# Output projection of a hybrid encoder layer as a Strassen product over pairs of T tiles

## The chip, the cores and the metric

The kernel runs on one core of a Trainium2 chip. The metric is device time in microseconds (us). Three runs of the kernel before took 2392.14 (median), 2390.62 and 2395.7 us. One more execution was profiled.

## The reference

One encoder layer in float32, T = 2048 tokens, width 1024, batch 1. The stages up to the FFN, cut:

```
hmix = rms_norm(x, g_norm1) * (1 + scale1) + shift1
q_a,k_a,v_a, q_m,k_m,v_m, o_m, gates = split(hmix @ w_in)
att = rms_norm(banded_attention(q_a, k_a, v_a, sink), g_attn_out)          # 512 columns
h_m = sigmoid(o_m) * rms_norm(h_fwd + h_bwd, g_mlstm_out)                  # 512 columns
mix = concatenate([att, h_m], axis=-1) @ w_out                             # [2048,1024] @ [1024,1024]
x   = x + gate1 * mix
hff = rms_norm(x, g_norm2) * (1 + scale2) + shift2
gte, up = split(hff @ w_ffn_in);  x = x + gate2 * ((silu(gte) * up) @ w_ffn_out)
out = rms_norm(x, g_final)
```

Only the line `mix`, the norm of `att` before it and the places around them are changed.

## The kernel before, in words

**Precision.** Each float32 product is made of three products on TensorE: an operand is split into a high part (a copy on ScalarE that rounds) and a low part (the difference, on VectorE or POOL), and `mm3` adds high x high, high x low and low x high (L56, L57, L58) into one PSUM bank of 128x512.

**Order of work.** TensorE's order is the one written in the code (a manual schedule); the other engines' instructions are put in order by a scheduler when the kernel is built, and each engine runs its own in order. DMAs are all issued from SP, one after the other; a DMA whose wait isn't met holds up those behind it. `fill` is a queue of generators; `pull(n)` runs n of their steps, so that products of one stage are woven between those of another.

**Stages.** The input projection and the mLSTM come first. Then attention: 32 steps (16 blocks of 128 tokens, 2 key heads). A step makes the scores on TensorE, the exponents on VectorE and ScalarE, the denominators on VectorE (L689, L691, L692), divides on POOL (L694, four instructions a step), transposes a step later on TensorE (L701) and multiplies by v (L713, L714). In between it pulls products of the o gate of the mLSTM (`gps`, L416). What attention leaves is written to DRAM (mxa_d), as the mLSTM's result (mxm_d) and the gate (og_d) had been.

**Output projection.** T is taken in tiles of 128 tokens, in the order TO: blocks of four tiles, the last block first. For each tile, `mix_load` loads attention's and the mLSTM's 512 rows each and the gate, squares attention on ScalarE and sums over four groups on VectorE (L893). `mix_scale` adds over partitions and broadcasts with one product with ones of 128x128 (L903), takes the inverse root on VectorE on 128x128, scales, gates (L905, L907) and splits (L911, L913). `out_proj` then makes 2 halves x 8 k x 3 = 48 products, adds each half onto x (L1028) and stores the tile (L1029; `x_d` in the rows). w_out times gate1 is loaded, multiplied on POOL (L926) and split while the remaining `gps` products run.

**The FFN's norm.** `norm2` loads four finished tiles (L954), sums squares on ScalarE (L149), takes the root on VectorE (`rsv`, `rsa`, `rsy`, 128x4), scales on ScalarE (L153), transposes on TensorE (L161) and writes the operands of the FFN's Strassen products to DRAM (hop_d). It is begun at tiles 5 and 9, for the blocks that ended with tiles 3 and 7. `load_ops` brings the operands back and splits them. The FFN itself multiplies in Strassen form already (`pair`, products `fp`).

Of the kernel before, what the change touches and what calls it, by code (L numbers as in the profile page):

```python
# [11 lines left out]
F32 = mybir.dt.float32  # L12
F32R = mybir.dt.float32r
# [23 lines left out]
def hybrid_layer_kernel(  # L37
# [36 lines left out]
    hop_d = dp.tile([2, 7, 4, P, 512], F32, name="hop_d")  # L74
    a_d = dp.tile([7, DFF // P // 2, P, 2, 512], F32, name="a_d")
# [770 lines left out]
    BO = tuple(reversed(range(NB)))  # L846
# [3 lines left out]
    fill.extend([o_tiles((h,), range(NB), []) for h in (0, 1)] + lasts)  # L850
    order = [(bi, kv) for kv in range(KV) for bi in range(NT)]
# [3 lines left out]
    for s_ in range(len(order) + 2):  # L855
# [14 lines left out]
        if u0:  # L870
            u0.normalize()
        pull(1)
# [4 lines left out]
        u2, u1 = u1, u0  # L877
    s3s.close()


    xp = ctx.enter_context(tc.tile_pool(name="xp", bufs=2, side="left", reuse_waits="tile"))
    mx = mxs.enter_context(tc.tile_pool(name="mx", bufs=2, side="right", reuse_waits="tile"))

    def mix_load(tt):
        raw = mx.tile([P, KT, P], F32, tag="mraw", name="mraw")
        sp.dma_start(raw[:, 0:4, :], mxa_d[tt].rearrange("(k p) t -> p k t", p=P))
        sp.dma_start(raw[:, 4:8, :], mxm_d[:, tt].rearrange("h p t -> p h t"))
        og = mx.tile([P, 4, P], F32, tag="og", name="og", bufs=1)
        sp.dma_start(og, og_d[tt].rearrange("h p t -> p h t"))
        sq = mx.tile([P, 4, P], F32, tag="msq", name="msq", bufs=1)  # L890
        act.activation(sq, raw[:, 0:4, :], AF.Square)
        ss = mx.tile([P, P], F32, tag="mss", name="mss", bufs=1)
        dve.tensor_reduce(ss, sq.rearrange("p k t -> p t k"), axis=mybir.AxisListType.X, op=ADD)  # L893
        return tt, raw, og, ss

    def load_xr(tt):
        xr = mx.tile([P, D], F32, tag="xr", name="xr")
        sp.dma_start(xr, x[tt * P:(tt + 1) * P, :])
        return xr

    def mix_scale(tt, raw, og, ss):
        ps = bank("b", "aps")
        pe.matmul(ps[:, :P], ones, ss, start=True, stop=True)  # L903
        r = rsqrt(mx, ps[:, :P], P, 512, "ar", 1)
        dve.scalar_tensor_tensor(raw[:, 4:8, :], og, 1.0, raw[:, 4:8, :], ADD, MUL)  # L905
        for k in range(4):
            dve.scalar_tensor_tensor(raw[:, k, :], raw[:, k, :], cols[:, O_GA + k:O_GA + k + 1], r, MUL, MUL)  # L907
        mh = mx.tile([P, KT, P], F32R, tag="mh", name="mh")
        ml = mx.tile([P, KT, P], F32R, tag="ml", name="ml")
        for ks in (slice(4, 8), slice(0, 4)):  # L910
            act.activation(mh[:, ks, :], raw[:, ks, :], AF.Copy)  # L911
        for e, ks in ((pool, slice(4, 8)), (dve, slice(0, 4))):
            e.tensor_tensor(ml[:, ks, :], raw[:, ks, :], mh[:, ks, :].bitcast(F32), SUB)  # L913
        return tt, mh, ml
# [3 lines left out]
    def w_out_half(j):  # L918

        js = slice(j * 512, (j + 1) * 512)  # L920
        wo.append(Kt(3 - j, f"wo{j}"))
        for k in range(0, KT, 2):
            r = xp.tile([P, 2, 512], F32, tag="xt", name="wor", bufs=4)
            sp.dma_start(r, w_out[k * P:(k + 2) * P, js].rearrange("(k p) c -> p k c", p=P))
            hi, lo = (wo[j].t[z][k // 2] for z in range(2))
            pool.tensor_tensor(r, r, g1b[:, js].unsqueeze(1).to_broadcast([P, 2, 512]), MUL)  # L926
            act.activation(hi, r, AF.Copy)
            dve.tensor_tensor(lo, r, hi.bitcast(F32), SUB)
            pull(11)
# [13 lines left out]
    while fill:  # L943
        pull()
# [498 lines left out]
```

## Time and profile before

| what | us |
|---|---|
| three runs, median (lowest, highest) | 2392.14 (2390.62, 2395.7) |
| profiled execution | 2391.88 |
| its span | 2390.1 |
| last attention product starts | 824.51 |
| first product of the output projection | 854.42 |
| first product of the FFN | 1074.21 |

The profile has a page of sums and views of the trace. In a timeline each row has a start, a duration, the engine, the line, the operation with what it writes and reads, and in brackets the idle time of the engine before it with what ended it. In a table by windows the columns are the window, the time TensorE was busy and its instructions, the same for its weight loads, VectorE, ScalarE and POOL, then the granted TensorE clock (1.00 is full speed), the busy share of the DMA engines and GB/s.

### The profile page before, as it was taken

Reading aid. Unit: us, or ns where it says so; the run is one execution under the profiler, and the core shown is the slowest. Engines: PE = TensorE matmul, PEld = TensorE weight load, DVE = VectorE, ACT = ScalarE, POOL = GpSimd, SP = SyncE. Lnnn points to the kernel's source line nnn. Section 1 sums busy time; section 2 is a strip of 40 time slices with the busy share of each in tenths; the row PEclk is TensorE's granted clock in tenths of the full one; section 3 lists DMA queues with packets and bytes.
Section 4 is the critical chain, followed back from the end, with each engine's and each line's share of the span. In section 5 each row is a group of like instructions: output and inputs, shape, how many; then the busy total and the mean of one; then the engine's idle time right before and its main releaser. Section 6 shows DMA issues by size and latency. Waiting matters only on the chain.

```text
span 2390.1 us, 32541 instructions
## 1 busy us (share of the span) xinstructions
PE 2273.7 (95%) x10865; PEld 1884.0 (79%) x10865; DVE 1586.3 (66%) x3162; ACT 1042.7 (44%) x2111; POOL 955.2 (40%) x786
## 2 busy tenths in 40 slices
PE   5988999999999989988999999999999999999998
PEld 4987777788888868777878778788888888888886
DVE  6775677667688786776556665755555636685594
ACT  4522555544578623434454333534433423323352
POOL 1001234334333341225655555555656545493020
PEclk9999999999999989999999999999999999999999
DMA  7574455576656556874343442533333354452462
GB/s 292 176 242 107 133 158 161 166 210 190 191 174 190 158 186 202 276 261 129 111 155 125 140 146 93 211 97 114 99 111 104 93 196 169 133 172 97 132 212 97
DMA packets 340721, 382.98 MB, mean 160 GB/s; under 512 B 23247, under 2 KB 234185, under 8 KB 340553
## 3 DMA queue, kind: packets, MB, share of 16 engines
q1 hardware_dynamic: 340552, 380.90, 50.4%
q8 instruction: 86, 1.41, 0.3%
q14 instruction: 83, 0.67, 0.1%
HBM read 268.97 MB, written 111.85 MB: 159 GB/s over the span
## 4 chain that ended last, share of the span: by engine, by line
PE 72%; DVE 10%; DMA 9%; issue 4%; ACT 2%; POOL 2%; SPq 1%; POOLq 0%; DVEq 0%; ACTq 0%
PE gps L416 10%; PE fp L56 10%; PE fp L57 10%; PE fp L58 10%; PE fo L56 6%; PE fo L57 6%; PE fo L58 6%; PE atp L701 2%; DMA bc<-bc_d 1%; DMA vst_d<-vs 1%; DVE macc L332 1%; PE ao L714 1%; PE as L678 1%; PE as L679 1%; PE ao L713 1%
## 5 line engine op out<-in xcount | busy, mean ns | idle before, releaser
L416 PE MATMUL gps<-hT,whi 128*128 128x512 f32 x1088 | 397.3, 420 | 7.0 <-ACT ctanh L430 7.0
L56 PE MATMUL fo<-w,ah 128*128 128x512 f32 x616 | 241.6, 392 | 0.0
L58 PE MATMUL fo<-w,al 128*128 128x512 f32 x616 | 241.4, 392 | 0.0
L57 PE MATMUL fo<-w,ah 128*128 128x512 f32 x616 | 241.4, 392 | 0.0
L416 PE MATMUL gps<-hT,wlo 128*128 128x512 f32 x544 | 228.3, 420 | 0.0
L416 PEld LDWEIGHTS gps<-hT,whi 128*128 128x128 f32 x1088 | 201.8, 191 | 32.3 <-ACT ctanh L430 7.4
L56 PE MATMUL fp<-T,S 128*128 128x512 f32 x528 | 208.7, 395 | 12.0 <-ACT u L1149 10.5
L58 PE MATMUL fp<-T,S 128*128 128x512 f32 x528 | 207.9, 394 | 0.0
L57 PE MATMUL fp<-T,S 128*128 128x512 f32 x528 | 207.9, 394 | 0.0
L1229 DVE TENSOR_TENSOR al<-al,ah 128x1024 fp32r<-128x1024 f32 x77 | 114.7, 1492 | 133.1 <-ACT ah L1228 132.9
L1061 DVE TENSOR_TENSOR A<-graw,A 128x512 fp32r<-128x512 f32 x86 | 108.6, 1282 | 130.9 <-ACT A L1060 130.9
L1228 ACT ACTIVATE ah<-al 128x1024 fp32r<-128x1024 f32 x77 | 81.6, 1060 | 189.3 <-DMA al<-a_d 186.4
L56 PE MATMUL fp<-B,A 128*128 128x512 f32 x352 | 138.4, 393 | 0.0
L58 PE MATMUL fp<-B,A 128*128 128x512 f32 x352 | 137.7, 391 | 0.0
L57 PE MATMUL fp<-B,A 128*128 128x512 f32 x352 | 137.6, 391 | 0.0
L56 PEld LDWEIGHTS fo<-w,ah 128*128 128x128 f32 x616 | 115.6, 188 | 26.5 <-ACT ah L1228 0.4
L57 PEld LDWEIGHTS fo<-w,ah 128*128 128x128 f32 x616 | 115.6, 188 | 26.1
L58 PEld LDWEIGHTS fo<-w,al 128*128 128x128 f32 x616 | 115.5, 188 | 26.1
L56 PEld LDWEIGHTS fp<-T,S 128*128 128x128 f32 x528 | 100.0, 189 | 36.4 <-ACT u L1149 12.7
L1061 DVE TENSOR_TENSOR S<-sf,S 128x512 fp32r<-128x512 f32 x86 | 91.7, 1067 | 49.0 <-ACT S L1060 48.9
L1065 POOL TENSOR_TENSOR sf<-A,A22r 128x512 f32<-128x512 f32 x43 | 63.4, 1475 | 148.0 <-DMA A<-in_w_ffn_in_dram 72.2
L694 POOL TENSOR_SCALAR ap<-ap,adn 128x384 f32<-128x384 f32 (+1 forms) x128 | 71.4, 578 | 126.1 <-DVE adn L692 61.4
(358 smaller groups left out, 6082.6 us busy)
## 6 DMA issues: line engine op xcount, KB each, us to landing
al<-a_d SPq DMA_DIRECT2D x77, 512.0 KB, 3.6
wmod<-in_w_mod_dram SPq DMA_DIRECT2D x48, 512.0 KB, 5.9
graw<-in_w_ffn_in_dram SPq DMA_DIRECT2D x43, 512.0 KB, 4.5
a_d<-ka SPq DMA_DIRECT2D x66, 256.0 KB, 2.1
bc<-bc_d SPq DMA_DIRECT2D x64, 256.0 KB, 4.2
a_d<-u SPq DMA_DIRECT2D x55, 256.0 KB, 2.7
mqk<-qk_d SPq DMA_DIRECT2D x48, 256.0 KB, 3.9
A<-in_w_ffn_in_dram SPq DMA_DIRECT2D x43, 256.0 KB, 3.2
```

The lines of the kernel that those rows point to most:

```text
L56: pe.matmul(o, lh, rh, start=first, stop=False, skip_group_check=skip)
L57: pe.matmul(o, lh, rl, start=False, stop=False, skip_group_check=skip)
L58: pe.matmul(o, ll, rh, start=False, stop=last, skip_group_check=skip)
L332: dve.scalar_tensor_tensor(acc, w[:, i, :], sc_col[:, k + i:k + i + 1], acc, MUL, ADD)
L416: pe.matmul(ps, w[i == 2][:, k, :], hT[n](i == 1, k), start=(k == 0 and i == 0), stop=(k == KT - 1 and i == 2))
L678: pe.matmul(s[:, :NK], self.q[:, g, :], self.kk[:, 0, :NK], start=True, stop=False)
L694: pool.tensor_scalar(self.p[g][:, :self.NK], self.p[g][:, :self.NK], dn[:, g:g + 1], 0.0, MUL, ADD)
L701: pe.transpose(tp[:, g * P:(g + 1) * P], self.p[g][:, i * P:(i + 1) * P], ident)
L1061: dve.tensor_tensor(t[:, 1, :], f, t[:, 0, :].bitcast(F32), SUB)
L1065: pool.tensor_tensor(f1, a21, a22, ADD)
L1228: act.activation(ah, al.bitcast(F32), AF.Copy)
L1229: dve.tensor_tensor(al, al.bitcast(F32), ah.bitcast(F32), SUB)
```

## The change

The output projection takes pairs of T tiles, in ascending order. The 2x2 blocks are (tile of the pair) x (attention or mLSTM half of the 1024 rows) and (half of the rows) x (half of the columns of w_out). Seven products of blocks, each 4 k x 3, replace eight. The sums on the side of w_out are made in advance by `w_out_ops`, in eight groups beside attention, and stored in wo_d; `load_wo` loads and splits the seven. The sums on the side of the tokens are made on POOL for each pair (`operands`). `out_proj` adds each product, in a PSUM bank that goes on adding, onto x.

The norm of attention sums squares on POOL, then two products with one column of ones give 128x2 (L960), the root is taken on 128x2, put on a diagonal, and a product with ones broadcasts it (L968). Loads, root, scale and splits for a pair stand between the products of the pair before. `norm2` for the first two blocks is begun at pairs 2 and 4, directly behind the pair that ends its block. The FFN's first operands are loaded and split inside the last pair by `refill_ops`, which is used later in the FFN too.

```diff
-    BO = tuple(reversed(range(NB)))
+    BO = tuple(range(NB))
...
+    def w_out_ops():
+        for c_ in range(2):
+            cs = slice(c_ * 256, (c_ + 1) * 256)
+            gb = wq.tile([P, 2, 256], F32, tag="gb", name="gb")
...
+            for k in range(4):
+                bx, by = (wq.tile([P, 2, 256], F32, tag=t, name=t) for t in ("bx", "by"))
...
+                yield True
+                ts = wq.tile([P, 4, 256], F32, tag="ts", name="ts")
+                dve.tensor_tensor(bx, bx, gb, MUL)
+                pool.tensor_tensor(by, by, gb, MUL)
+                pool.tensor_tensor(ts[:, 1, :], bx[:, 1, :], bx[:, 0, :], SUB)
+                pool.tensor_tensor(ts[:, 2, :], by[:, 1, :], bx[:, 1, :], SUB)
+                pool.tensor_tensor(ts[:, 0, :], by[:, 1, :], ts[:, 1, :], SUB)
+                pool.tensor_tensor(ts[:, 3, :], by[:, 0, :], ts[:, 0, :], SUB)
+                yield True
+                for u, t in ((0, bx[:, 0, :]), (1, by[:, 0, :]), (5, by[:, 1, :]), (2, ts[:, 0, :]),
+                             (3, ts[:, 1, :]), (4, ts[:, 2, :]), (6, ts[:, 3, :])):
+                    sp.dma_start(wo_d[u, k][:, cs], t)
+                yield True
...
         if u0:
             u0.normalize()
+        if s_:
+            next(wops, None)
...
-        dve.tensor_reduce(ss, sq.rearrange("p k t -> p t k"), axis=mybir.AxisListType.X, op=ADD)
...
+        def sums(self):
+            self.sq = sq = mring_tile("msq", F32).rearrange("p i (k t) -> p i k t", k=4)
+            act.activation(sq, self.a, AF.Square)
+            pool.tensor_tensor(sq[:, :, 0:2], sq[:, :, 0:2], sq[:, :, 2:4], ADD)
+            pool.tensor_tensor(sq[:, :, 0], sq[:, :, 0], sq[:, :, 1], ADD)
+            dve.scalar_tensor_tensor(self.m, self.og, 1.0, self.m, ADD, MUL)
+        def root(self):
+            self.ps = ps = bank("c", "aps")
+            for i in range(2):
+                pe.matmul(ps[:, i:i + 1], self.sq[:, i, 0], ones[:, 0:1], start=True, stop=True)
+            r = rsqrt(mx, ps[:, :2], 2, 512, "ar", 1)
+            for i in range(2):
+                dve.tensor_scalar(self.sq[:, i, 1], ident, r[:, i:i + 1], None, MUL)
+        def scale(self):
+            rb = self.ps[:, 128:384].rearrange("p (i t) -> p i t", i=2)
+            for i in range(2):
+                pe.matmul(rb[:, i], ones, self.sq[:, i, 1], start=True, stop=True)
+            for k in range(4):
+                dve.scalar_tensor_tensor(self.a[:, :, k], self.a[:, :, k], cols[:, O_GA + k:O_GA + k + 1], rb, MUL, MUL)
+        def operands(self):
...
+            pool.tensor_tensor(a21, a11, a21, SUB)
+            pool.tensor_tensor(s2_, a22, a21, SUB)
+            part(a11, "mA11")
...
     finish_fill(lasts[0])
-    g1b = wp.tile([P, D], F32, tag="wraw", name="g1b", bufs=1)
...
+    nxt = Pair(0)
+    load_wo(range(2))
+    nxt.sums()
+    pull(6)
     finish_fill(lasts[1])
+    load_wo(range(2, 4))
+    nxt.root()
+    pull(12)
+    nxt.scale()
+    ready = nxt.operands()
+    next(ready), next(ready)
...
-        if tt in (5, 9):
-            norms.append(norm2(0, (tt - 5) // 4, "cd"))
...
+        if p in (2, 4):
+            norms.append(norm2(0, p // 2 - 1, "bd"))
...
-        for i in range(16):
+        for i in range(28):
             pull(1)
...
+                if i == 2:
+                    nxt.sums()
+                elif i == 7:
+                    nxt.root()
+                elif i == 13:
+                    nxt.scale()
+                    ready = nxt.operands()
+                elif i in (15, 18, 21):
+                    next(ready)
```

How the change moves instructions is seen at three places. First SP at the end of attention, before: attention's last stores (L719), then the first tile's loads (L886, L887).

```order
L489 DMA og_d<-oth 128x4x128
L719 DMA mxa_d<-at 64x4x128 x2
L489 DMA og_d<-oth 128x4x128
L719 DMA mxa_d<-at 64x4x128 x2
L886 DMA mraw<-mxa_d 128x4x128
L887 DMA mraw<-mxm_d 128x4x128
```

And after; L720 is attention's store, L1004 a part of w_out, L942 and L944 the first pair's loads:

```order
L720 DMA mxa_d<-at 64x4x128
L945 DMA og<-og_d 128x8x128
L720 DMA mxa_d<-at 64x4x128
L490 DMA og_d<-oth 128x4x128
L720 DMA mxa_d<-at 64x4x128 x2
L1004 DMA wo<-wo_d 128x2x512 x2
L942 DMA ma<-mxa_d 128x8x128
L944 DMA mm<-mxm_d 128x4x128 x2
```

Two w_out loads now stand between the last store of attention and the first load of the norm.

Second, VectorE where the FFN's norm takes its root (rsv, rsy, rsh, rsa on 128x4, for the first block), before:

```order
L98 TENSOR_SCALAR rsv<-ssq 128x4
L99 TENSOR_SCALAR rsy<-rsv 128x4
L100 TENSOR_SCALAR rsh<-rsv 128x4
L1028 TENSOR_TENSOR xr<-xr,ops 128x512
L102 TENSOR_TENSOR rsa<-rsy 128x4
L905 SCALAR_TENSOR_TENSOR mraw<-og,mraw 128x512
L98 TENSOR_SCALAR arv<-aps 128x128
L103 TENSOR_TENSOR rsa<-rsa,rsh 128x4
```

And after, in pair 2 (mA and mS are operands of pair 3, L979 the low part of one, which needs ScalarE's high part first):

```order
L103 TENSOR_TENSOR rsa<-rsy 128x4
L1021 TENSOR_TENSOR xr<-xr,ops 128x512
L104 TENSOR_TENSOR rsa<-rsa,rsh 128x4
L979 TENSOR_TENSOR mA_10925<-ma,mA_10925 128x512
L105 SCALAR_TENSOR_TENSOR rsy<-rsa,rsy 128x4
L979 TENSOR_TENSOR mS_11006<-ma,mS_11006 128x512
L103 TENSOR_TENSOR rsa<-rsy 128x4
L979 TENSOR_TENSOR mS_10959<-ms_10922,mS_10959 128x512
L104 TENSOR_TENSOR rsa<-rsa,rsh 128x4
L979 TENSOR_TENSOR mS_11009<-mm,mS_11009 128x512
L105 SCALAR_TENSOR_TENSOR rsy<-rsa,rsy 128x4
L979 TENSOR_TENSOR mS_11003<-ma,mS_11003 128x512
```

Between two steps of the root now stands a low part of an operand.

Third, TensorE in pair 2 of the kernel after (mS names the stationary operand of a product; the transposes of the FFN's norm are L162):

```order
L968 MATMUL aps<-msq,ones_r 128x128 x2
L56 MATMUL ops<-wo,mS_10777 128x512
L57 MATMUL ops<-wo,mS_10777 128x512
L58 MATMUL ops<-wo,mS_10777 128x512
...
L56 MATMUL ops<-wo,mS_10780 128x512
L57 MATMUL ops<-wo,mS_10780 128x512
L58 MATMUL ops<-wo,mS_10780 128x512
L162 MATMUL trn<-ident,x1t 128x128 x4
L56 MATMUL ops<-wo,mS_10780 128x512
```

The transposes stand 54 products and the norm's small ones behind the pair's start, and that pair follows directly on the one that finished the block; before, a whole tile of 48 products lay between.

191 lines of the change are left out of this document (102 added, 89 removed).

## The prediction

> **What bounds the kernel now.** I read the page's busy table and chain of waits first, then the windows by stage, then TensorE's timeline from the last attention product to the FFN.
>
> ```profile
> span 2390.1 us, 32541 instructions
> PE 2273.7 (95%) x10865; PEld 1884.0 (79%) x10865; DVE 1586.3 (66%) x3162; ACT 1042.7 (44%) x2111; POOL 955.2 (40%) x786
> PE 72%; DVE 10%; DMA 9%; issue 4%; ACT 2%; POOL 2%; SPq 1%; POOLq 0%; DVEq 0%; ACTq 0%
> ...
> 700.00:760.00 60.00, 60.00 (x340) 51.68 (x339) 48.99 (x146) 46.99 (x129) 24.40 (x41) 1.00 0.59 178
> 854.40:874.00 19.60, 11.33 (x34) 8.65 (x35) 19.36 (x20) 5.13 (x6) 10.84 (x4) 0.68 0.45 140
> 950.00:1000.00 50.00, 47.08 (x209) 36.49 (x208) 34.06 (x89) 24.64 (x35) 7.11 (x5) 0.97 0.86 275
> ```
>
> TensorE is busy 95% of the span, and in attention (700 to 760) 60.00 us of 60. So work taken from it pays one for one, and any wait put in front of it costs one for one. In 854.4 to 874 it stands for 8 us, and the granted clock is 0.68. The stage of the change, with the idle time before each row in brackets:
>
> ```profile
> 824.51 0.40 PE L714 MATMUL ao<-aptl,av 128*128 128x512 f32 x1
> 832.07 0.46 PE L903 MATMUL aps<-mss,ones_r 128*128 128x128 f32 x2 [1.25 <-DVE mss L893]
> 854.42 0.50 PE L56 MATMUL ops<-wo,mh 128*128 128x512 f32 x1 [2.15 <-ACT oth L488]
> 870.32 0.79 PE L57 MATMUL ops<-wo,mh 128*128 128x512 f32 x1 [8.25 <-DVE wo L928]
> 1038.04 0.79 PE L56 MATMUL ops<-wo,mh 128*128 128x512 f32 x1 [7.10 <-ACT mh L911]
> 1074.21 0.39 PE L56 MATMUL fp<-B,A 128*128 128x512 f32 x1
> 1094.42 0.79 PE L56 MATMUL fp<-T,S 128*128 128x512 f32 x1 [6.68 <-ACT u L1149]
> ```
>
> The projection runs from 854.42 to 1074.21, 219.8 us; 824.51 is the last attention product and 1074.21 the FFN's first. Starts of successive products give their price:
>
> ```profile
> 849.62 0.39 PE L416 MATMUL gps<-hT,whi 128*128 128x512 f32 x1
> 851.43 0.62 PE L416 MATMUL gps<-hT,whi 128*128 128x512 f32 x2
> 871.34 0.63 PE L56 MATMUL ops<-wo,mh 128*128 128x512 f32 x1
> 874.32 0.63 PE L57 MATMUL ops<-wo,mh 128*128 128x512 f32 x1
> 905.76 0.40 PE L58 MATMUL ops<-wo,ml 128*128 128x512 f32 x1
> 907.86 0.39 PE L58 MATMUL ops<-wo,ml 128*128 128x512 f32 x1
> 936.75 0.39 PE L58 MATMUL ops<-wo,ml 128*128 128x512 f32 x1
> 937.65 0.39 PE L57 MATMUL ops<-wo,mh 128*128 128x512 f32 x1
> 1074.89 0.39 PE L56 MATMUL fp<-B,A 128*128 128x512 f32 x1
> ```
>
> Fill products: 8 steps in 1.81 us, 0.227 us each. Old projection: 9 steps in 2.10 us, 0.2333. FFN products: 3 steps from 1074.21 to 1074.89, 0.227. After a stop: 7 steps in 2.98 us, 0.426 each; some 12 products run so, hence a restart costs about 12 x 0.19 = 2.3 us. Between 936.75 and 937.65 lie two projection steps and four transposes, so such a group costs 0.90 - 0.47 = 0.43.
>
> **TensorE's work.** Before: 16 tiles x 48 = 768 products, 179.2 us at 0.2333. After: 8 pairs x 7 x 4 x 3 = 672. Their stationary operand is now sliced out of a two-part tile exactly as in the FFN's products, so I take 0.2275: 152.9 us; at the other row's price it would be 156.8. The 16 groups of transposes stay (6.9 us); the norm's own small products come to about 0.6 us a pair, 4.2 for the seven pairs inside the projection. Together 164.0 us without any wait, where 190.6 stood before (179.2, 6.9 and about 4.5): 26.6 us less. Of the old 219.8 us, 29.2 were stops and restarts. The question is how many of these come back.
>
> **The front.** The rows that price the norm of the first pair:
>
> ```profile
> 826.96 0.55 SPq L886 DMA_DIRECT2D mraw<-mxa_d  x1
> 830.24 0.63 ACT L891 ACTIVATE msq<-mraw 128x512 f32<-128x512 f32 x1 [1.00 <-DMA mraw<-mxa_d]
> wor<-in_w_out_dram SPq DMA_DIRECT2D x8, 512.0 KB, 5.1
> L927 ACT ACTIVATE wo<-wor 128x1024 fp32r<-128x1024 f32 x8 | 8.3, 1055 | 12.8 <-POOL wor L926 12.8
> L986 POOL TENSOR_TENSOR n2w<-n2w 128x512 f32<-128x512 f32 x4 | 5.3, 1324 | 13.3 <-DVE n2w L985 13.3
> ```
>
> Before, 26 fill products stand between the last attention product and the norm's first (L903), and TensorE waited only 1.25 us. Now 16 stand there (to 824.74 + 16 x 0.2275 = 828.4), and the load of attention's output (L942) is queued on SP behind two w_out loads (L1004) that wait until the fill has left their buffers at 828.4. Two issues of 0.55 bring SP to 829.6; 512 KB in 5.1 us land at 834.7. ScalarE has those two w_out parts to split first (the first lands about 833.7; 2 x 1.06, to 835.8), then squares 1024 elements (1.06, to 836.9); POOL adds 512 (1.32) and 256 elements (0.75, an estimate: half of 1.32 and a start), to 839.0. TensorE waits 10.7 us. Bounds: 8, if the loads land as fast as the 256 KB at 826.96 did, and 13.
>
> Then a restart (2.3) and 83 fill products (18.9) lead to the first product of the projection at 860.4. The second product's operand stands on ScalarE behind w_out splits whose loads can only be issued when fill buffers come free, at about 852 to 854, so that they land by 859.5: four splits and a square of 1.06 and five copies of about 0.6 end near 868, and TensorE wants the operand at 863.2. That is 5 us more. Effective start: 865.4, against 854.42 with 29.2 us of stops to come.
>
> **The FFN norm of blocks 0 and 1.** The chain from a tile's last addition to its transposes, as it ran before:
>
> ```profile
> 915.39 0.68 DVE L1028 TENSOR_TENSOR xr<-xr,ops 128x512 f32<-128x512 f32 x1
> 920.14 0.43 SPq L954 DMA_DIRECT2D x1t<-x_d  x1
> 924.66 1.06 ACT L149 ACTIVATE junk<-x1t 128x1024 bf16<-128x1024 f32 x1 [2.46 <-DMA x1t<-x_d]
> 925.84 0.17 DVE L98 TENSOR_SCALAR rsv<-ssq 128x4 f32<-128x4 f32 x1 [2.92 <-ACT junk L149]
> 932.24 2.19 ACT L153 ACTIVATE x1t<-x1t,rsy 128x1024 f32<-128x1024 f32 x2 [5.11 <-DVE rsy L104]
> 936.98 0.60 PE L161 MATMUL trn<-ident,x1t 128*128 128x128 f32 x4
> ```
>
> 21 us from the addition's end (about 916.0) to 936.98; TensorE didn't wait, because a whole tile of products lay between. Now the block's last addition is the end of one pair, and the transposes stand 54 products and two small ones into the next: 12.9 us later. Addition to rsv takes 9.8 us; with 0.9 for the addition and a junk queued behind other work, rsv runs at about 11.6. Its root is no longer a run of small instructions: on VectorE each of its steps stands behind one operand difference of the next pair, and those wait for ScalarE's copies, which wait for four sums on POOL (4 x 1.32 = 5.3, after the scale at 12.6). The last copy is done at 18.5; two differences of 0.69 and the rest of the root, to 20.6; four scalings on ScalarE (2.19 for two, 4.5 with a start) end at 25.2 to 26. TensorE waits 13 us in pair 2 and, with one more 1024-element instruction of VectorE between, 14 in pair 4, each with a restart: 31.6 us. Bounds: 5 each if the root slips through (the same chain without its 6.4 us of root, less 12.9), 16 each if the loads are slower.
>
> The other pairs have 4.1 us (18 products) from the norm's root to its use, for about 3.3 us of small VectorE steps; I put 2 us over all pairs, 0 to 6.
>
> First FFN product: 865.4 + 164.0 + 31.6 = 1061.0, plus 2 = 1063, against 1074.21: 11 us gained. In the FFN's first pair the operand splits move into the last projection pair, but the transposes of the next block still stand there behind ScalarE's queue: I take 1 us less than the 6.68, between 8 less and 3 more.
>
> **Attention.** Eight groups of w_out sums are made beside it:
>
> ```profile
> 742.91 2.29 POOL L694 TENSOR_SCALAR ap<-ap,adn 128x384 f32<-128x384 f32 x4 [4.09 <-DVE adn L692]
> 745.68 0.60 PE L701 MATMUL atp<-ident,ap 128*128 128x128 f32 x4
> 747.74 0.16 DVE L691 TENSOR_TENSOR adn<-adn,ars 128x4 f32<-128x4 f32 x1 [0.93 <-ACT adn L690]
> ...
> 927.21 1.48 POOL L913 TENSOR_TENSOR ml<-mraw,mh 128x512 fp32r<-128x512 f32 x1 [10.58 <-ACT mh L911]
> 927.67 1.05 DVE L103 TENSOR_TENSOR rsa<-rsa,rsh 128x4 f32<-128x4 f32 x1
> ```
>
> A group is one product of 512 elements and four differences of 256 on POOL, 1.32 + 4 x 0.75 = 4.3 us, put right behind a step's normalisation. POOL is idle 4.09 us there, and its results are used 0.48 us after they are done (745.20 to 745.68). So the next normalisation comes 0.2 us late by length alone. The last two rows show more: a 128x4 step that takes 0.15 to 0.17 elsewhere took 1.05 while POOL ran a sum. The denominators of the softmax (L689, L691) are such steps, and now meet POOL busy: 0.5 to 1 us later. Over eight groups I take 5 us, from 0 to 20. The 12 MB of added transfers over some 150 us (80 GB/s) raise the DMA share from 0.59 to about 0.86, which the window 950 to 1000 had as well; SP's loads for attention are issued a step ahead, and I take nothing for it.
>
> The Trainium skill, GPSIMD Engine Reference, section 8 (Key points), says that GpSimd shares its SBUF interfaces with VectorE and contends with instructions that read two SBUF inputs; that speaks against the change, and the 1.05 us agrees. By that rule alone every denominator step would wait out a POOL instruction, about 1.3 us twice in each of eight steps, some 20 us by these rows instead of the 5.
>
> **Sum.** Against the profiled 2391.88 (its span and 1.8 us around it): -11 (projection) - 1 (FFN) + 5 (attention) = -7, 2384.9. That run lies 0.26 under the median, so I forecast 2385.
>
> **Rivals.** *The root slips through* (0.10): the scheduled order holds but the copies are early, both stalls fall to about 5: 16 us less, 2369. Against it: the four POOL sums can't start before the scale. *The FFN gap closes* (0.10): with the operands split inside the last pair, the 6.68 and its restart go too: 8 us less, 2377. *The gain is eaten* (0.25): products at 0.2333 (+4) and stalls of 15 each (+3): 2392. For it: 0.2333 was this stage's price. *Attention pays* (0.17): the mechanism above at 2.5 us a group, 20 us instead of 5: 2400. It decides from 1.5 us a group on (12 us use up the 12 of projection and FFN); against it, POOL's idle 4.09 nearly holds a group.
>
> **How the numbers follow.** The forecast itself has 0.38; its own range is 2377 to 2393. A difference under 0.2%, 4.8 us, is about what a measurement of this kernel can't tell from none (the three runs spread over 5). Faster: 0.25 of the forecast's 0.38, both early rivals, and 0.03 elsewhere, 0.48. Same: 0.11, 0.16 and 0.03 of the others, 0.30. Slower: 0.22. The 8 in 10 range takes in the closed gap and most of the attention rival: 2371 to 2402.
>
> **What would show it.** TensorE idle about 11 us before L960 of the first pair, some 5 us before its second product, and 13 to 14 us before L162's transposes in pairs 2 and 4, put down to ScalarE's scaling; 0.227 us between products; windows of attention with a little under 60 of 60. Stalls under 7 us at the transposes, or attention over 15 us longer, would prove me wrong.

## The result: the change made the kernel 1.4% slower

Four runs of the kernel after took 2428.66 us in the median (2424.51 to 2433.65), four runs of the kernel before on the same chip 2393.92 (2390.62 to 2400.79). The ratio is 1.0142, with a 95% interval from 1.0111 to 1.0174. The forecast of 2385, its range and its likeliest sign were wrong.

The profiled execution of the kernel after took 2426.65 us, its span is 2424.8. Cut at the same four places as before (the starts of the last attention product, of the first projection product and of the first FFN product, and the end), the two traces differ so, in us:

| stretch | before | after | difference | forecast |
| --- | --- | --- | --- | --- |
| start to last attention product | 824.51 | 842.27 | +17.8 | +5 |
| from there to the first projection product | 29.9 | 39.2 | +9.3 | +6.0 |
| projection | 219.8 | 222.3 | +2.5 | -17.2 |
| first FFN product to the end | 1315.9 | 1321.0 | +5.1 | -1 |
| sum | 2390.1 | 2424.8 | +34.7 | -7.2 |

In the forecast's column 6.0 is 860.4 - 824.51 - 29.9, and -17.2 is 1063 - 860.4 - 219.8. Every stretch came out worse than forecast; attention by 12.8 and the projection by 19.7 are the large ones. From the page of the kernel after, the busy line and the shares of its chain of waits:

```profile
PE 2271.7 (94%) x10801; PEld 1875.9 (77%) x10801; DVE 1593.7 (66%) x3104; ACT 1062.6 (44%) x2133; POOL 1014.2 (42%) x850
...
PE 68%; DMA 10%; DVE 9%; issue 5%; ACT 4%; POOL 3%; SPq 1%; POOLq 0%; ACTq 0%; DVEq 0%
```

TensorE has 64 instructions fewer, but hardly less busy time, and its share of the chain fell from 72 to 68%. POOL gained 59 us of work. TensorE's timeline after, at the places that the forecast named:

```profile
842.27 0.39 PE L715 MATMUL ao<-aptl,av 128*128 128x512 f32 x1
...
856.40 1.01 PE L960 MATMUL aps<-ones_r,msq 128*128 128x1 f32 x4 [9.89 <-POOL msq L953]
...
884.52 0.39 PE L57 MATMUL ops<-wo,mA 128*128 128x512 f32 x1
...
886.78 0.39 PE L58 MATMUL ops<-wo,mA 128*128 128x512 f32 x1
...
888.78 0.47 PE L56 MATMUL ops<-wo,mS 128*128 128x512 f32 x1 [1.27 <-DVE xr L1021]
...
943.98 0.39 PE L58 MATMUL ops<-wo,mS 128*128 128x512 f32 x1
955.66 0.47 PE L162 MATMUL trn<-ident,x1t 128*128 128x128 f32 x1 [11.30 <-ACT x1t L154]
...
958.91 0.77 PE L56 MATMUL ops<-wo,mS 128*128 128x512 f32 x1
...
1019.42 0.48 PE L162 MATMUL trn<-ident,x1t 128*128 128x128 f32 x1 [10.31 <-ACT x1t L154]
...
1120.14 0.69 PE L162 MATMUL trn<-ident,x1t 128*128 128x128 f32 x2 [7.98 <-ACT x1t L154]
```

The three stops that were forecast are there: 9.89 us before the norm's first product (10.7 forecast), 11.30 and 10.31 at the transposes; with the three further pauses of 0.56 between the transposes, TensorE does no products for 14.7 us (944.21 to 958.91; forecast 13). Ten steps from 884.52 to 886.78 make 0.226 us a product. What was missed lies elsewhere.

**Attention.** The same stretch, first to last product, by windows (columns as before), first before, then after:

```profile
618.98:824.51 205.53, 205.48 (x1140) 177.16 (x1141) 164.57 (x479) 159.22 (x428) 78.60 (x131) 0.99 0.60 177
```

```profile
620.12:842.27 222.15, 212.13 (x1139) 176.06 (x1140) 178.97 (x490) 163.16 (x432) 113.60 (x171) 0.99 0.77 227
```

Of POOL's 35.0 us more, 33.9 are the eight groups, 4.2 each, as forecast (4.3). The stretch begins 1.1 us later and is 16.6 longer: TensorE stands for 10.0 us where it stood for 0.05, and its 1139 instructions take 6.7 us more. Beside loads of the keys (3.7 us), it waited for these (us in total, times, longest):

```profile
PE ao L715 <- DVE aptl L124: 5.3, 9, 1.6
PE as L679 <- DVE aptl L124: 1.2, 2, 0.7
PE atp L702 <- POOL ap L695: 1.0, 3, 0.6
```

One group of sums in the timeline after, POOL first (`by`, `bx`, `ts` are the sums), then VectorE, then TensorE:

```profile
673.02 0.74 POOL L871 TENSOR_TENSOR ts<-bx 128x256 f32<-128x256 f32 x1 [1.96 <-DVE bx L869]
...
676.59 0.74 POOL L874 TENSOR_TENSOR ts<-by,ts 128x256 f32<-128x256 f32 x1
677.32 2.29 POOL L695 TENSOR_SCALAR ap<-ap,adn 128x384 f32<-128x384 f32 x4
...
690.77 0.69 DVE L869 TENSOR_TENSOR bx<-bx,gb 128x512 f32<-128x512 f32 x1 [2.63 <-DMA bx<-in_w_out_dram]
691.45 0.68 DVE L124 TENSOR_TENSOR aptl<-atp,apth 128x512 fp32r<-128x512 f32 x1
...
692.19 0.50 PE L715 MATMUL ao<-aptl,av 128*128 128x512 f32 x1 [1.63 <-DVE aptl L124]
```

Two things are seen. The normalisation (L695) starts at the instant the group ends, with no idle time of POOL before it. And a product by the gate that VectorE holds (L869) waits 2.63 us for its load, with the low part of the attention weights (L124) behind it, for which TensorE then waits 1.63. The denominators, by groups, before and after:

```profile
L689 DVE TENSOR_TENSOR adn<-nmx,skb 128x4 f32<-128x4 f32 x32 | 6.4, 201 | 0.6
...
L691 DVE TENSOR_TENSOR adn<-adn,ars 128x4 f32<-128x4 f32 x32 | 5.0, 157 | 2.6 <-ACT adn L690 2.3
```

```profile
L690 DVE TENSOR_TENSOR adn<-nmx,skb 128x4 f32<-128x4 f32 x32 | 11.7, 365 | 0.5
...
L692 DVE TENSOR_TENSOR adn<-adn,ars 128x4 f32<-128x4 f32 x32 | 6.5, 203 | 3.0 <-ACT adn L691 2.9
```

Not all of the 16.6 us is lost beside the sums. Counted from the first score product, attention's products run 11.3 us later than before at 774, when the groups are done (the last at 769). They keep that distance until 821 and lose 5.3 more in the last nine products. There VectorE splits the first parts of w_out (L1006), which before were split from 844 on, behind attention. POOL's last normalisation before, then one of the splits, that normalisation and the transposes after:

```profile
818.14 1.85 POOL L694 TENSOR_SCALAR ap<-ap,adn 128x256 f32<-128x256 f32 x4 [1.97 <-DVE adn L692]
...
830.40 1.22 DVE L1006 TENSOR_TENSOR wo<-wo 128x1024 fp32r<-128x1024 f32 x1
835.08 2.63 POOL L695 TENSOR_SCALAR ap<-ap,adn 128x256 f32<-128x256 f32 x4 [6.27 <-DVE adn L693]
836.40 1.74 PE L702 MATMUL atp<-ident,ap 128*128 128x128 f32 x4 [0.58 <-POOL ap L695]
```

The denominators stand on VectorE behind such splits; POOL waits 6.27 us for them where it waited 1.97, and TensorE then waits for POOL.

**The root of the FFN's norm.** VectorE after, in pair 2, two sums of the operands on POOL beside it, and the scaling on ScalarE that follows:

```profile
946.82 0.68 DVE L979 TENSOR_TENSOR mA<-ma,mA 128x512 fp32r<-128x512 f32 x1
946.96 1.67 POOL L984 TENSOR_TENSOR ms<-mm,ma 128x512 f32<-128x512 f32 x1
947.42 1.22 DVE L105 SCALAR_TENSOR_TENSOR rsy<-rsa,rsy 128x4 f32<-128x4 f32 x1
948.56 0.68 DVE L979 TENSOR_TENSOR mS<-ma,mS 128x512 fp32r<-128x512 f32 x1
948.70 1.66 POOL L991 TENSOR_TENSOR mm<-mm,ms 128x512 f32<-128x512 f32 x1
949.16 1.22 DVE L103 TENSOR_TENSOR rsa<-rsy 128x4 f32<-128x4 f32 x1
...
954.47 2.19 ACT L154 ACTIVATE x1t<-x1t,rsy 128x1024 f32<-128x1024 f32 x2 [1.70 <-DVE rsy L105]
```

This is the forecast's picture: each step of the root stands behind one operand difference, and the chain ends in ScalarE's scaling. Two of the steps shown last 1.22 us, for four elements a partition; they end at 948.64 and 950.38, where POOL's sums end (948.63 and 950.36).

**The rest of the projection.** All that TensorE waited for between 881.5 and 1103.8 after (what waited, for what: us in total, times, longest):

```profile
PE trn L162 <- ACT x1t L154: 25.0, 8, 11.3
PE ops L56 <- DVE xr L1021: 6.8, 5, 2.2
PE aps L968 <- DVE msq L963: 5.7, 4, 2.3
PE aps L960 <- POOL msq L953: 1.6, 1, 1.6
```

The last three rows, 14.1 us, are short waits in all pairs. In the second, the PSUM bank of a product isn't free because the addition onto x (L1021) that reads it is late. The third and fourth, 7.3 us, are the norm of attention for the next pair.

### The profile page after: what moved, and what is told of

It is laid out like the page before. It is cut to its first block, busy times and chain, and to the rows that moved or that the text cites. A ratio compares the mean times of both kernels' runs of the same rounds, so it can differ in the third digit from the quotient of the medians.

```text
span 2424.8 us, 32609 instructions
## 1 busy us (share of the span) xinstructions
PE 2271.7 (94%) x10801; PEld 1875.9 (77%) x10801; DVE 1593.7 (66%) x3104; ACT 1062.6 (44%) x2133; POOL 1014.2 (42%) x850
## 4 chain that ended last, share of the span: by engine, by line
PE 68%; DMA 10%; DVE 9%; issue 5%; ACT 4%; POOL 3%; SPq 1%; POOLq 0%; ACTq 0%; DVEq 0%
PE fp L56 10%; PE fp L57 10%; PE fp L58 10%; PE gps L417 9%; PE fo L56 6%; PE fo L58 6%; PE fo L57 6%; DMA bc<-bc_d 1%; DMA vst_d<-vs 1%; DMA x1t<-x_d 1%; PE trn L162 1%; PE atp L702 1%; DVE macc L333 1%; DMA graw<-in_w_ffn_in_dram 1%; DVE S L1141 1%
## 5 line engine op out<-in xcount | busy, mean ns | idle before, releaser
L56 PEld LDWEIGHTS fp<-T,S 128*128 128x128 f32 x528 | 100.0, 189 | 32.5 <-ACT u L1242 7.4
L58 PEld LDWEIGHTS fp<-T,S 128*128 128x128 f32 x528 | 99.9, 189 | 22.1
```

Source lines behind the costliest of these rows:

```text
L56: pe.matmul(o, lh, rh, start=first, stop=False, skip_group_check=skip)
L58: pe.matmul(o, ll, rh, start=False, stop=last, skip_group_check=skip)
```

## The experiments

The theory at the start of the experiments: the sums on POOL cost attention its 17.8 us, the norm's position costs the stops at the transposes, and VectorE's queue in the projection makes the short waits. The rivals: the added transfers are what attention pays for; VectorE's own product by the gate is; the stops hide other waits, so that their removal gains nothing. Line numbers are those of the kernel that ran. Where only one run was made, differences under 5 us, about the spread of a kernel's runs, say nothing.

### The sums: all, transfers alone, arithmetic alone

`e1` leaves out all sums and their stores and reads the seven operands' bytes from another buffer of the same size; `e2` keeps every transfer and leaves out the arithmetic; `e3` loads one group once, does the arithmetic eight times on it, stores nothing, and reads the operands as `e1` does. In all three the projection therefore works on other numbers than w_out's.

```diff
 e1
-        if s_:
-            next(wops, None)
 e2
-                dve.tensor_tensor(bx, bx, gb, MUL)
-                pool.tensor_tensor(by, by, gb, MUL)
-                pool.tensor_tensor(ts[:, 1, :], bx[:, 1, :], bx[:, 0, :], SUB)
...
 e3
-                    sp.dma_start(wo_d[u, k][:, cs], t)
```

> The changed kernel without the eight groups of w_out sums beside attention: nothing is loaded, multiplied, subtracted or stored for them, and the seven parts of w_out are read at the same places and in the same sizes from another tensor in DRAM (so the projection multiplies other numbers). In the changed kernel the last attention product starts at 842.3 us, before at 824.5. Theory A (the sums beside attention cost the 17.8 us): it starts at 824 to 827, and the whole is 15 to 18 us shorter than the changed kernel, about 2410. Rival (attention became longer for another reason, such as the ascending order or the order of the fill): it stays over 835, and the whole changes by less than 7 us.

> The changed kernel with the transfers of the w_out sums and without their arithmetic: the same loads and the same 56 stores (of unsummed pieces), no instruction on VectorE or POOL. Last attention product, 842.3 in the changed kernel and 824.5 before. Theory A1 (POOL's and VectorE's instructions make attention longer): 825 to 830. Theory A2 (the 80 GB/s of transfers and their 100 issues on SP make attention's own loads late): 837 to 842. If both matter, between.

> The changed kernel with the arithmetic of the w_out sums and without their transfers: one group is loaded once, the eight groups run on it, nothing is stored, and the seven parts are read from another tensor of the same size. Last attention product, 842.3 in the changed kernel. Theory A1 (arithmetic): 835 to 841. Theory A2 (transfers): 825 to 830. VectorE's 128x4 steps of the denominators (430 ns on average in the changed kernel, 214 before) stay near 430 under both.

| kernel | time | last attention product |
| --- | --- | --- |
| before (trace) | 2391.88 | 824.51 |
| after (trace) | 2426.65 | 842.27 |
| no sums | 2409.79, ratio 1.0084 [1.0066, 1.0102] | 824.78 |
| transfers alone | 2413.11 (one run) | 829.00 |
| arithmetic alone | 2427.32 (one run) | 847.66 |

Without the sums attention ends where it did before; with the transfers alone 4.5 us later, with the arithmetic alone 23 us later. The scheduler had put two groups into one step there, so 23 is not the arithmetic's price in the kernel after; but it settles that the arithmetic pays and the transfers little.

Attention itself is not as short as before, though. Without the sums it starts at 614.28, 4.7 us earlier than before, for which no run shows the reason, and takes 210.5 us, against 205.5 before and 222.2 after. So 11.7 of its 16.6 us more go with the sums, and 5.0 stay; 3.8 of these are lost in the last nine products, where the splits of w_out stand in this kernel too. And 1.0084 is left without any sums, 15.0 us by the trace: about half of the loss lies behind attention.

### VectorE's product moved to POOL

```diff
-                dve.tensor_tensor(bx, bx, gb, MUL)
+                pool.tensor_tensor(bx, bx, gb, MUL)
```

> The changed kernel with the one instruction of each group of w_out sums that ran on VectorE (the product bx, 0.69 us) moved to POOL. In the changed kernel it waited for its load at the head of VectorE's queue, 2.6 us once, with the softmax's denominators behind it, and attention's last product started at 842.3 us. Theory A3 (VectorE's queue is held up by that instruction): under 832. Theory A4 (POOL's sums stand in front of the next normalisation, whoever multiplies): 840 or more, since POOL now has 5.6 us a group in place of 4.3.

It took 2426.05 us (one run), with attention's end at 843.62. The stop of L869 seen above was real, but taking it away gained nothing: TensorE's waits in attention for VectorE's low parts fell from 6.5 to 3.4 us, and those for POOL's normalisation rose from 1.0 to 5.9.

### The sums spread over attention

A group's six operations, all on POOL, are spread over three of attention's steps, and POOL's order is the one written in the code.

```diff
+    hp_.enter_context(tc.manual_schedule(engines={mybir.EngineType.Pool}))
...
                 pool.tensor_tensor(by, by, gb, MUL)
+                yield True
                 pool.tensor_tensor(ts[:, 1, :], bx[:, 1, :], bx[:, 0, :], SUB)
                 pool.tensor_tensor(ts[:, 2, :], by[:, 1, :], bx[:, 1, :], SUB)
+                yield True
```

> The same arithmetic and the same transfers, all arithmetic on POOL, but spread: POOL's order is held as written during attention, with two products behind one normalisation, two differences behind the next and two behind the one after (2.6, 1.5 and 1.5 us, each below the 4.09 us that POOL was idle per step in the kernel before). Theory A4 (a group's length between two normalisations is what costs): attention's last product starts at 826 to 831 and the whole is 11 to 16 us shorter than the changed kernel, about 2406 to 2411. Rival (the total of POOL's work or the shared access of POOL and VectorE costs): it stays at 837 or more.

It took 2429.68 us, ratio 1.0171 [1.0146, 1.0196], no better. Attention ended at 847.68. Its denominators take 216 and 202 ns in the mean, the first back from 365, so that lengthening isn't what costs. TensorE's waits in attention of this kernel:

```profile
PE gps L417 <- DMA ak<-kst_d: 5.4, 1, 5.4
PE gps L417 <- POOL wlo L231: 5.2, 2, 3.4
```

POOL also makes the low part of the fill products' weights (L231), 2.4 us each, and with POOL's order fixed in this way those are late; in the kernel after TensorE never waited for them in attention. So the next run moved them:

```diff
-        pool.tensor_tensor(lo, r, hi.bitcast(F32), SUB)
+        dve.tensor_tensor(lo, r, hi.bitcast(F32), SUB)
```

> As the spread sums (POOL's order held as written), and the low parts of the fill's weights (L231, 2.4 us each on POOL) are made on VectorE. With the spread sums alone attention's last product started at 847.7 us, and 10.6 us of TensorE's idle time there stood before fill products that waited for these low parts behind other work of POOL. Theory A4 (only a long piece of POOL's work between two normalisations costs): without these waits it starts at 826 to 832. Rival (POOL's total, or its access shared with VectorE, costs also when spread): 836 or more.

2405.91 us (one run): some 24 gained. Part of it comes ahead of attention, whose first score product starts at 608.61 in place of 618.77; attention itself takes 215.7 us in place of 228.9, against 205.5 before the change.

### The sums made in the mLSTM stage

If it is only attention that has no room on POOL, the sums are free in the stage ahead of it, where POOL is busy 66 us of 300. The groups, of half the columns each, all on POOL, are pulled in the mLSTM's backward loops.

```diff
         for cc in list(range(NT - 1, 0, -1)) + [0, 0]:
             tick()
+            if cc > 3:
+                next(wops, None)
```

> The changed kernel with the same sums made earlier, in the mLSTM stage, 128 columns at a time, all on POOL, none beside attention. If the sums cost attention its 17.8 us only because POOL's normalisation is on attention's chain: the last attention product starts at 825 to 829 and the whole is 13 to 18 us shorter than the changed kernel, 2407 to 2412. Rival (the same 34 us of POOL's work costs wherever it stands, since the mLSTM uses POOL too): attention begins later by 8 us or more, and the whole gains under 8.

2442.09 us, ratio 1.0229 [1.0211, 1.0247]: worse. Attention takes 209.9 us but starts at 649.47. Windows of the mLSTM stage, before, then of this kernel:

```profile
100.00:400.00 300.00, 274.46 (x1549) 238.33 (x1549) 201.13 (x598) 125.78 (x338) 66.49 (x76) 0.99 0.54 154
```

```profile
100.00:400.00 300.00, 259.91 (x1424) 226.30 (x1423) 189.62 (x528) 112.65 (x296) 105.38 (x149) 0.95 0.62 176
```

POOL does 39 us more, and TensorE gets 125 instructions fewer done. Idle time on POOL, counted over a stage, isn't room. The transfers came along (the DMA share, the column before the last, rose from 0.54 to 0.62), and no run separates their part from the arithmetic's here.

### The FFN's norm one pair later

```diff
-        if p in (2, 4):
+        if p in (3, 5):
             norms.append(norm2(0, p // 2 - 1, "bd"))
```

> The changed kernel with the FFN's norm of blocks 0 and 1 begun at pairs 3 and 5 in place of 2 and 4, nothing else. In the changed kernel TensorE stands 14.7 and 13.7 us at its transposes. Theory B (only the missing slack of a pair makes these stops): both fall under 1 us, with their restarts some 30 us go, and the whole is about 2397. Rival (VectorE and ScalarE can't hold the norm and the operands, so the stop moves to the operands or the FFN's start): the projection gets less than 15 us shorter, and new idle time stands before products of the pairs or at the FFN's first pair.

2412.01 us, ratio 1.0087 [1.0069, 1.0106]. The stops at the transposes are gone and the projection takes 207.0 us in place of 222.3, but 28.4 were to be had (14.7 and 13.7). The waits for the additions onto x rose from 6.8 to 17.8, by the view of TensorE's waits:

```profile
PE ops L56 <- DVE xr L1021: 17.8, 8, 7.0
```

The longest of them in the timeline, ScalarE, VectorE and TensorE:

```profile
1067.46 0.63 ACT L1140 ACTIVATE S<-sf 128x512 fp32r<-128x512 f32 x1 [5.69 <-POOL sf L1145]
...
1068.12 1.20 DVE L1141 TENSOR_TENSOR S<-sf,S 128x512 fp32r<-128x512 f32 x1 [1.81 <-ACT S L1140]
1069.47 1.52 DVE L1141 TENSOR_TENSOR S<-A,S 128x512 fp32r<-128x512 f32 x1
1070.91 1.47 DVE L1021 TENSOR_TENSOR xr<-xr,ops 128x512 f32<-128x512 f32 x2
...
1071.73 0.77 PE L56 MATMUL ops<-wo,mS 128*128 128x512 f32 x1 [6.96 <-DVE xr L1021]
```

In the last pair an addition that frees a bank stands on VectorE behind two differences of the FFN's first operands, one of which waits for ScalarE, which waits for a sum on POOL. To see that it is the queue, the next kernel leaves the low parts of the operands out (L979) and multiplies the high part in their place, so that TensorE has as many products:

```diff
-                dve.tensor_tensor(t[:, 1, :], f, t[:, 0, :].bitcast(F32), SUB)
...
-                mm3(ps, w[:, 0, ks], w[:, 1, ks], ...
+                mm3(ps, w[:, 0, ks], w[:, 0, ks], ...
```

> As the run with the norm one pair later, and VectorE's low parts of the seven operands of each pair are left out (the products take the high part twice, so the same number of products with other values). With the norm later, TensorE stood 17.8 us waiting for VectorE to add a product onto x before its PSUM bank could be used again (L1021), 7.0 us at most at once. Theory C (VectorE's queue, filled by the operands' low parts which wait for POOL's sums, delays the emptying of the bank): these waits fall under 5 us and the projection from 207 to 192 or less. Rival (a product's bank is simply needed again too soon, 12 products or 2.8 us later, whatever VectorE does): over 10 us of them stay.

2390.68 us (one run), projection 186.5 us, and the waits for the additions:

```profile
PE ops L56 <- DVE xr L1020: 5.5, 4, 2.1
```

So some 20 us of the projection hang on VectorE's differences, 12.3 of them as waits for the additions, which stand in the same queue. This is the one run that shows what the seven products would bring: 219.8 - 186.5 = 33 us, the stops of the kernel before included, if VectorE's 56 differences cost nothing.

A combination with a later norm in the FFN as well (the second half's norm begun one step later, `n > 1`) and the spread sums:

> Three remedies together in the changed kernel: the sums spread as above, the FFN's norm of blocks 0 and 1 begun one pair later, and the FFN's norm of the second half begun one unit later (its transposes stood in the FFN's first unit, and TensorE waited 8.0 us for them). If the three causes are separate and add: -14 (attention), -15 (projection, as measured with the norm later), -6 (FFN), about 2392, no different from the kernel before. If they overlap (the FFN's first unit stays short of operands): 2398 to 2405.

2419.29 us, ratio 1.0122 [1.0093, 1.0151], later than either side expected. Attention ended at 848.92, as late as with the spread sums alone. The projection took 203.6, but from the FFN's first product to the end it was 1328.2, where the norm's move alone had 1324.7: no gain from beginning later.

### The first pair's root later, and three remedies at once

```diff
     load_wo(range(2, 4))
+    pull(36)
     nxt.root()
```

> The changed kernel with the first pair's root 36 steps of the fill later, nothing else. In the changed kernel TensorE waited 9.9 us before L960, and 39.2 us lay between the last attention product and the first of the projection. If that wait is only a matter of how many fill products stand before it: under 1 us is left and the 39.2 become 26 to 29. Rival (the stop moves to the first pair's operands): 34 to 39 us with a new stop before the first products of the projection.

2413.94 us (one run). The stop before L960 is 0.20 us in place of 9.89, and the stretch to the first projection product 28.6 in place of 39.2. The projection gave 4.6 back (226.9); the stretch from the FFN on was 6.3 shorter, for which I have no reason. Both differences are about as large as the spread of a kernel's runs.

With the sums in the mLSTM stage, the norm later and the root later:

> The sums in the mLSTM stage, the FFN's norm of blocks 0 and 1 one pair later, and the first pair's root 36 steps of the fill later (the stop before L960 was 9.9 us). By the parts so far: -16 (sums), -15 (projection) and +3 (FFN), -12 (front with its restart): about 40 us less than the changed kernel, 2383 to 2390, at least as fast as the kernel before. Rival (the front's stop only moves, to the first operands, because their chain now has 36 products less to hide behind): 2393 to 2400.

2421.0 us, ratio 1.0138 [1.0122, 1.0154], again later than either side expected: 21 us off the kernel with the sums in the mLSTM stage, for front and projection, while attention still starts 32 us later than before.

### All remedies, and the kernel before with one of them

The last three kernels ask whether the losses add up, and what the move of the fill weights' low part is worth by itself (L226 in the expectation is L230 in the rows). The first kernel has the spread sums, the fill weights on VectorE, the norm a pair later and the root later; the second is the kernel before with the fill weights on VectorE alone; the third is the first with two of the seven differences of a pair on POOL.

> Sums spread over attention on POOL, the fill weights' low part on VectorE, the FFN's norm one pair later, the first root 36 products later. If the four losses are separate, their gains add: 2405.9 (the first two remedies together) less about 12 (the norm a pair later, as measured alone) less about 6 (the root, what was left of its 10.6 after the pairs gave 4.6 back): about 2388, level with the kernel before. Rival: the projection's VectorE queue holds the end in every form, so what one remedy frees another wait takes back (as in the run with three remedies at once): 2396 or more, with waits before L1028 (the additions onto x) above 20 us in all.

> The kernel before with one edit: the low part of the fill weights (L226) on VectorE in place of POOL. If the last 10 us by which attention is longer with spread sums (215.7 against 205.5) are the sums' own cost, then attention keeps its 205 to 206 us here and starts about 10 us earlier, as it did with this edit in the changed kernel: about 2378 to 2382. Rival: this edit itself lengthens attention (VectorE then carries the fill's splits beside the softmax), attention 212 to 216 us here, and the time is 2386 to 2394.

> The kernel with all remedies, and two of the seven operand low parts of a pair (of S1 and S4) on POOL in place of VectorE. If VectorE's queue in the projection is what is left over, its waits before the additions onto x (L1028) fall to half or less and the projection becomes 8 or more shorter than without this edit. Rival: POOL's subtractions hold up VectorE's two-operand steps as the w_out sums did, so that the projection changes by less than 3 us or becomes longer.

| kernel | time | ratio to before |
| --- | --- | --- |
| all remedies | 2389.60 | 1.0004 [0.9988, 1.0019] |
| before, fill weights on VectorE | 2382.44 | 0.9966 [0.9952, 0.9980] |
| all remedies, two low parts on POOL | 2404.49 | 1.0058 [1.0037, 1.0079] |

The four remedies add up as expected (2388). Attention of the second kernel takes 206.5 us (610.53 to 817.00), that of the first 215.6 (610.44 to 826.02).

The edit by itself leaves attention nearly as it was and starts it 8.4 us earlier, so it isn't what makes attention 9 us longer with the spread sums. Nor are the sums all of that: in the three kernels without sums beside attention (no sums, sums in the mLSTM stage, three remedies) it takes 210.5, 209.9 and 209.7 us, 4 to 5 more than before. The second kernel also beats both kernels of the comparison, though it has nothing to do with the change. Against it, the kernel with all remedies loses 9.0 us up to the last attention product, gains 1.5 in front of the projection and 9.8 in it (208.9 against 218.7), and loses 8.2 in the FFN (1323.7 against 1315.5), 6 us in all.

The third kernel answers the queue in the wrong direction. A group of differences on VectorE and one on POOL in its projection, and its waits for the additions:

```profile
L986 DVE TENSOR_TENSOR mA<-mm,mA 128x512 fp32r<-128x512 f32 x14 | 17.8, 1284 | 1.5 <-ACT mA L985 1.2
...
L986 POOL TENSOR_TENSOR mS<-mm,mS 128x512 fp32r<-128x512 f32 x8 | 13.5, 1687 | 0.0
```

```profile
PE ops L56 <- DVE xr L1028: 22.8, 9, 8.0
```

In the kernel with all remedies that VectorE group took 916 ns in the mean and the waits were 13.7 us. With two differences in seven taken off its queue, VectorE became slower at what was left (all its differences in the projection: 1.09 us in the mean, then 1.29), and the projection 15 us longer (224.1). In sum VectorE spent less on its differences, 48.9 us in place of 57.7, so its total doesn't explain the longer waits; what does is not shown.

## Why the prediction was wrong

**Attention: mis-sized, 5 against 17.8.** The step that failed is the argument that POOL's idle 4.09 us "nearly holds a group". It weighed one gap of one step on POOL against one group. In the kernel after, TensorE waited only 1.0 us for the normalisation, but 6.5 for VectorE's low parts, whose queue also held the product by the gate: VectorE stood idle 7.5 us before the eight of them, for their loads, which the forecast had put at nothing. With that product on POOL the normalisation was waited for 5.9 us, and attention was no shorter. So a group held TensorE up whichever of the two engines made that product. A second term was put at nothing as well: the splits of w_out were counted only for the front, and they stand in attention's last nine products, which lost 5.3 us.

The rival *Attention pays* had the right place, and its 20 us came near the 17.8. That is in part luck: the sums' share inside attention is 11.7 us, 1.5 a group and not 2.5. The lengthened denominators that were to carry the 5 us are real (11.7 us against 6.4, and 6.5 against 5.0), but the spread version has the first of them nearly as short as before and is no faster.

The Trainium skill, GPSIMD Engine Reference, section 8 (Key points), was quoted with 20 us by its rule, nearer to the 17.8 than the forecast. The trace doesn't show it by the path that was costed for it: the denominators grew by 6.8 us in all. Where it shows directly is the root of the FFN's norm: the steps of 1.22 us read two inputs on 128x4 and end with POOL's sums.

**The front: right in sum, wrong in its parts.** Forecast 35.9 us to the first projection product, measured 39.2. The stop was 9.89 (10.7). The fill products behind it were some 97 and not 83, 3.2 us, a miscount; and the 5 us before the second product didn't come (1.27 at 888.78). Inside the stop two errors cancel, which is luck. The first pair's load (L942) was issued 3.6 us after the last attention product and not 5.1, since SP was held by attention's last stores (to 844.63) and not by the fill's buffers; and it landed 6.4 us later and not 5.1.

**TensorE's work: right.** It is 0.226 us a product, and the rival with 0.2333 falls, apart from some stretches at that price.

**The stops at the transposes: right,** 14.7 and 13.7 against 13 and 14, with the chain as foretold, down to the root between the differences. Moving the norm took them away.

**The other pairs: the step that failed in the projection.** "I put 2 us over all pairs" became 14.1. The forecast asked only when the norm's root would be ready, and that alone came to 7.3, above its bound of 6. It didn't ask for the additions that free the PSUM banks, which stand in the same VectorE queue as the differences; they cost the other 6.8, and 17.8 with the norm later. A product needs its bank as it needs its operand, and a pair has three banks for seven products.

The longer stops are then paid a second time in TensorE's clock:

```profile
950.00:1000.00 50.00, 40.43 (x173) 32.18 (x174) 23.85 (x48) 20.69 (x28) 13.43 (x10) 0.82 0.57 179
1000.00:1050.00 50.00, 36.00 (x160) 28.62 (x160) 30.00 (x72) 17.90 (x25) 17.98 (x12) 0.83 0.63 217
```

The granted clock (third column from the end) is 0.82 and 0.83 there. In the timeline of the projection 43 product steps took 0.40 to 0.45 us, 0.2 more than the others, 8.6 us; the forecast had 4.6 for two restarts. In this trace they follow the stops of 1.56, 1.99, 2.21, 2.28, 10.31 and 11.30 us, five to ten steps each; behind the six stops of 0.60 to 1.32 there are none. Of the 19.7 by which the projection missed, 12.1 are these waits, 4.0 the clock and 1.4 the stops at the transposes; 5 counted for the second product weren't needed. That leaves some 7 us that I can't place.

**FFN: -1 forecast, +5.1 measured.** The stop of 6.68 became 7.98 at 1120.14 and some smaller ones. Over the runs of the changed kernel this stretch took from 1314.7 to 1328.2 us. Which of its waits the change itself makes isn't settled.

## What to carry to other kernels

Before work is moved to an engine that looks half idle, list everything else on that engine and its neighbours which TensorE waits for, and add the delay for each; the busy share alone says little (66 us of 300 in the mLSTM stage, and attention started 30 us later). Count PSUM banks as operands: the instruction that empties a bank is as critical as the one that fills the next operand, and should not stand behind instructions that wait for other engines. And a product scheme with fewer multiplications pays in VectorE and POOL work: here the projection was 33 us shorter only with the low parts left out.

## What the runs showed of the hardware that I had not expected

Moving work from VectorE to POOL made what stayed on VectorE slower: two differences of 128x512 moved to POOL took 1.6 to 1.7 us there, and VectorE's other ones went from 1.09 to 1.29 in the mean, with a projection 15 us longer. This agrees with the Trainium skill, Perfetto Trace Analysis, section Optimizing Scalar/DVE Operations, which doubts that offloading between the two helps because of their common port. But the direction matters. The fill weights' low part, in the kernel before and in that with the one edit (lowest, median and highest duration in ns):

```profile
L230 POOL TENSOR_TENSOR wlo<-wraw,whi x17: 2368/2395/2928, 134.8 to 777.3; 128x1024 fp32r<-128x1024 f32 x17
```

```profile
L230 DVE TENSOR_TENSOR wlo<-wraw,whi x17: 1210/1226/1734, 137.3 to 769.0; 128x1024 fp32r<-128x1024 f32 x17
```

Moved from POOL to VectorE it takes half as long, and the kernel before became 0.34% faster.
